# Gate and up of a hybrid decoder block: where the seven-product groups stand between the plain blocks

## The chip, the cores and the metric

The kernel runs on one core of one Trainium2 chip. The metric is the time on the device in microseconds (us), as the median of several executions. TensorE (PE) multiplies, VectorE (DVE) and ScalarE (ACT) prepare weights and take results out of PSUM, SyncE (SP) and GpSimd (POOL) issue transfers.

## The reference

One decoder layer on 256 tokens with 16 meta tokens in front, all in float32. The change lies in its last part, the gated feed-forward part:

```python
gate, up = jnp.split(_rms(h, n2) @ w_gu, 2, axis=-1)
return h + (jax.nn.silu(gate) * up) @ w_dn
```

`h` is 256 x 2048 here, `w_gu` is 2048 x 11264 (5632 columns of gate, 5632 of up) and `w_dn` is 5632 x 2048. All that comes before (RWKV-7 time mixing, forgetting attention, the gated merge and the output projection) stays as it is.

## The kernel before, in words

**Split weights.** Each float32 weight is turned into a high part `wh` (ACT copies and rounds it, line 343 or 518) and a low part `wl` (DVE subtracts the high part from the raw value, line 344 or 519). Activations are split the same way. A product is then three matmuls: high by high, high by low, low by high.

**Gate and up are cut into 11 strips of 512 columns.** Strips 0 to 7 (`PLAIN`) are done plainly. A strip has 8 gate blocks and then 8 up blocks (`plain_jobs`, `cm_jobs`). One plain block loads 256 rows of 512 weight columns and issues 16 matmuls on PE (lines 448, 449 and 451). So there are 128 plain blocks, numbered 0 to 127: gate of strip j is 16j to 16j+7 and up of strip j is 16j+8 to 16j+15. The 8 blocks of one gate or up add into four banks of PSUM, named `gt` or `up`, from the pool `main_ps`. After the last of the 8, `halves` (lines 455 and 456) takes the four banks out, and the next 8 blocks can open them again: this is what the title of the change calls a change of banks.

**Strips 8 to 10 (`BLOCK`) use a scheme with seven products** in place of eight on 2 x 2 sub-blocks (`block_jobs`). Gate of such a strip is one group (`bg8`, `bg9`, `bg10`), up another (`bh8`, `bh9`, `bh10`). A group goes through 8 channel pairs, and each pair is two pieces: a first piece with 9 matmuls (weights `fh`, `fl`) and a second one with 12 (weights `wh`, `wl` made from the raw tile `fr`), so 16 pieces in all. A group adds into four banks of the other pool, `aux_ps`; the first piece uses two of them, the second piece the other two. The second operands are sums of activations kept in eight tiles, `home0` to `home3` and four that lie in the rooms of the results of strips 6 and 7 (`homeh6`, `homel6`, `homeh7`, `homel7`, for channel pairs 4 to 7).

**After an up group** the function `turn` multiplies by the gate on DVE, then on PE transposes the result into two banks `bt` of the same pool `aux_ps` (line 403), and ACT and DVE split these into `ach` and `acl` (lines 518 and 519). Only then are the two banks free again. A pool gives a bank to a tile when its first instruction comes in the order of the program. The steps of `turn` are put off by a nominal clock (`LATER`, `FOLD`) which the matmuls move on, so they land some blocks later in the order.

**The table `SPANS` sets the order.** It has a row for each of the six groups: the plain block in front of which the first piece stands, the one in front of which the last piece stands, and the blocks that get no piece. Between these, one piece stands in front of each plain block. All five engines run in the order in which the program is written there (`manual_schedule`), and weights are made three jobs ahead of their matmuls (`AHEAD`), out of four buffers each for `wh` and `wl`.

**The down projection** comes after block 127. It adds the plain part into four banks `dn` (from `main_ps`) and the products of its own seven-product scheme into four banks `dnp` (from `aux_ps`), which are opened some 96 matmuls later. Up of strip 7 (`up7`, blocks 120 to 127) takes its banks from `aux_ps`, unlike the other strips.

Of the kernel before, what the change touches and what calls it, by code (L numbers as in the profile page):

```python
# [20 lines left out]
NMETA = 16  # L21

T = 256
# [4 lines left out]
DFF = 5632  # L28
# [13 lines left out]
for _n, _k in (("n1", 16), ("mu", 24), ("mu_w", 1), ("mu_a", 1), ("mu_g", 2), ("w0", 8), ("a0", 8), ("k_k", 8),  # L42
# [30 lines left out]
QUICK = [FAST[:-1], FAST]  # L73
PLAIN = list(range(8))
BLOCK = list(range(8, 11))
SPANS = ((8, 26, (11, 17, 21)), (28, 43, ()), (45, 62, (51, 59)), (64, 80, (75,)), (82, 99, (85, 93)),
         (101, 116, ()))
FOLD = 6000
AHEAD = 3
LATER = 2500  # L80
# [43 lines left out]
def hybrid_block(ctx, tc, A, out, dbg=None):  # L124
# [1329 lines left out]
    def plain_jobs(j):  # L1454
        gs = []
        rb = bcast(rsb2, 4)

        def post_gate(pss):
            g = gates_of(j)
            gs.append(g)  # L1460
            for m in range(4):
                halves(g[:, m], pss[m])

            def rest():
                nc.vector.tensor_tensor(g, g, rb, op=ALU.mult)
                yield LATER
                nc.scalar.activation(g, g, AF.Silu)
            spawn(rest(), LATER)

        def post_up(pss):  # L1470
            ub = gu.tile([P, 4, T], F32, tag="ub", name=f"ub{j}")
            for m in range(4):
                halves(ub[:, m], pss[m])

            def rest():
                nc.vector.tensor_tensor(ub, ub, gs[0], op=ALU.mult)
                yield LATER
                split(*act_of(j), ub)
                for i in range(2):
                    if 2 * j + i in FAST:  # L1480
                        yield (i + 1) * LATER
                        shape = "p (a n c) -> p a n c"
                        sr = room("l", BLOCK[-1], f"ss{2 * j + i}r", F32R).rearrange("p m c -> p (m c)")
                        ssd[2 * j + i] = yield from sums_of_tokens(sr.rearrange(shape, a=2, n=4), f"ss{2 * j + i}",
                                                                   ub[:, 2 * i], ub[:, 2 * i + 1], False)
            spawn(rest(), LATER)
        return (cm_jobs(wgu[:, j * 512:(j + 1) * 512], KT, hts, NMETA, T, post_gate, name=f"gt{j}")
                + cm_jobs(wgu[:, DFF + j * 512:DFF + (j + 1) * 512], KT, hts, NMETA, T, post_up, alloc=aux_ps if j == PLAIN[-1] else main_ps, name=f"up{j}"))

    def token(i, k, t):  # L1490
        at = NMETA + t * P
# [2 lines left out]
    def block_jobs(j):  # L1494
        gbs = []

        def group(col, post, name):
            box = []

            def mk(i):  # L1500
                src = wgu[i * 256:(i + 1) * 256, col + j * 512:col + (j + 1) * 512]
                first, end = i == 0, i == KT // 2 - 1
                raws = []

                def load0():
                    raw = gu.tile([P, 1024], F32, tag="fr", name="fr", bufs=2)
                    raws.append(raw)
                    rn = raw.rearrange("p (n c) -> p n c", c=256)
                    for k, to in enumerate((rn[:, 0::3], rn[:, 1:3])):
                        nc.sync.dma_start(to, src[k * P:(k + 1) * P, :].rearrange("p (x c) -> p x c", x=2))  # L1510
                    w = [gu.tile([P, 784], F32R, tag=t, name=t)[:, c:c + 768] for t, c in zip(("fh", "fl"), PLACE_T)]
                    split(*w, raw[:, :768])
                    b11, b21, b22, b12 = (raw[:, n * 256:(n + 1) * 256] for n in range(4))
                    nc.vector.tensor_tensor(rn[:, 0::3], rn[:, 0::2], bcast(b12, 2), op=ALU.subtract)
                    for o, x_, y_, op in ((b22, b22, b11, ALU.add), (b21, b21, b22, ALU.subtract)):
                        nc.vector.tensor_tensor(o, x_, y_, op=op)  # L1516
                    return w

                def load1():
                    w = [wp.tile([P, WCOLS], F32R, tag=t, name=t, bufs=WB)[:, c:c + 1024]  # L1520
                         for t, c in zip(("wh", "wl"), PLACE_T)]
                    split(*w, raws[0])
                    return w

                def product(at, a, w, n, opens=False, closes=False):
                    o = box[0][at]
                    hi, lo_ = (x_[:, n * 256:(n + 1) * 256] for x_ in w)
                    nc.tensor.matmul(o, a[0], hi, start=first and opens, stop=False, skip_group_check=True)
                    nc.tensor.matmul(o, a[1], hi, start=False, stop=False, skip_group_check=True)
                    nc.tensor.matmul(o, a[0], lo_, start=False, stop=end and closes, skip_group_check=True)  # L1530
                    slot(3 * 256 / 2.4)

                def s_of(n):
                    return tuple(homes[i][:, a, n, :] for a in range(2))

                def mul0(w):
                    if first:
                        b = [aux_ps(f"{name}{n}") for n in range(4)]
                        box.append({n: b[c // 2][:, (c % 2) * 256:(c % 2 + 1) * 256]
                                    for c, n in enumerate(("p1", "c12", "c11", None, "p7", "p5", "p6", "c21"))})  # L1540
                    product("p1", token(i, 0, 0), w, 0, True)
                    product("c12", s_of(3), w, 2, False, True)
                    product("c11", token(i, 1, 0), w, 1, True, True)

                def mul1(w):
                    product("p7", s_of(2), w, 3, True)
                    product("p5", s_of(0), w, 0, False, True)
                    product("p6", s_of(1), w, 2, True)
                    product("c21", token(i, 1, 1), w, 1, False, True)
                    if end:  # L1550
                        post(box[0])
                return [(load0, mul0), (load1, mul1)]
            return [mk(i) for i in range(KT // 2)]

        def sums(dst, ps, name):
            u, v = (gu.tile([P, 256], F32, tag=n, name=f"{name}{n}") for n in ("bu", "bv"))
# [20 lines left out]
        def post_up(ps):  # L1577
# [13 lines left out]
                for b, pt in enumerate(pts):  # L1591
                    split(*(t[:, 2 * b:2 * b + 2] for t in act_of(j)), pt.rearrange("p (m t) -> p m t", m=2))
            spawn(turn(), LATER)
        return [group(0, post_gate, f"bg{j}"), group(DFF, post_up, f"bh{j}")]

    def nudge(w):
        lo_ = w[0][1]
# [74 lines left out]
    def slow_jobs(i, cg, cs, end):  # L1672
        def mk(x_):
# [4 lines left out]

            def mul(w):
                if not cs:  # L1680
                    cs.extend(main_ps(f"dn{cg}{n}") for n in range(4))
                first = i == ORDER[cg][0]
                for t in range(2):
                    for k in range(2):
                        product(cs[2 * t + x_], a_of(i, k, t), w[0], k, first and k == 0, end and k == 1)
                    if end:
                        post(cg, t, x_, cs[2 * t + x_])
# [9 lines left out]
    def fast_jobs(i, cg, q, cs, ps, end):  # L1697
# [31 lines left out]

        def mul0(w):  # L1730
            if not ps:
                ps.extend(aux_ps(f"dnp{cg}{n}") for n in range(4))
            product(ps[0], a_of(i, 0, 0), w, 0, first, end)

        def mul1(w):
# [139 lines left out]
```

## Time and profile before

| | |
|---|---|
| median of 3 executions | 1523.97 us |
| the profiled execution, its own time | 1523.83 us |
| its span, first to last instruction | 1521.8 us |
| PE busy | 1500.7 us, 99% of the span |
| DVE busy | 1238.4 us, 81% |
| ACT busy | 842.3 us, 55% |
| first plain matmul of gate, first of down | 788.3 us, 1286.1 us |

Times in the rows are counted from the start of the span. Gate and up are the stretch from 788.3 to 1286.1 us. A row of the timeline gives the start, the duration, the engine and line, what is written and read, and, in square brackets, how long the engine stood idle in front of it and what ended that. A row of the waits gives who waited for whom, the sum, the number and the longest one.

### The profile page before, as it was taken

What the parts mean: (1) busy time and instruction counts of PE and PEld (TensorE: products, weight loads), DVE (VectorE), ACT (ScalarE), POOL (GpSimd) and SP (SyncE); (2) the same over time, 40 slices, a digit from 0 to 9 for tenths busy, and PEclk for the clock granted to TensorE, in tenths of its full rate; (3) what the DMA queues carried; (4) which work ended last, traced back from release to release, by engine and by line L of the source; (5) the groups of instructions that cost most, each with busy time, mean ns of one, the idle gap of its engine ahead of it and who ended that gap; (6) DMA issues with size and microseconds to landing.
All of it is one profiled execution on the core that took longest, in us unless ns stands there. A gap on an engine that the chain in (4) does not pass through costs nothing. (4 is left out here: it accounts for less than half of the span.)

```text
span 1521.8 us, 27095 instructions
## 1 busy us (share of the span) xinstructions
PE 1500.7 (99%) x10320; PEld 1344.1 (88%) x10320; DVE 1238.4 (81%) x2121; ACT 842.3 (55%) x1212; POOL 148.5 (10%) x263
## 2 busy tenths in 40 slices
PE   9999999999999999999999999999979999999998
PEld 9999999999989888998889999899969898887887
DVE  7888699689689757876777888889878986789987
ACT  7664565475465545544555555455545555555553
POOL 2112202302202100000002000000000001310000
PEclk9999999999999999999999999999989999999999
DMA  8567456646645757767879656476556656986662
GB/s 272 165 171 207 118 157 187 173 121 174 187 130 154 218 149 220 234 223 242 263 251 328 194 180 222 153 243 205 189 166 198 224 187 208 367 254 201 225 211 84
DMA packets 225123, 306.45 MB, mean 201 GB/s; under 512 B 26017, under 2 KB 148401, under 8 KB 224993
## 3 DMA queue, kind: packets, MB, share of 16 engines
q1 hardware_dynamic: 208960, 277.25, 59.1%
q0 software_dynamic: 9984, 20.98, 4.2%
q10 hardware_dynamic: 6048, 6.49, 1.2%
q8 instruction: 81, 1.33, 0.3%
q14 instruction: 50, 0.40, 0.1%
HBM read 285.90 MB, written 18.78 MB: 200 GB/s over the span
## 5 line engine op out<-in xcount | busy, mean ns | idle before, releaser
L344 DVE TENSOR_TENSOR wl<-raw,wh 128x1024 fp32r<-128x1024 f32 x402 | 490.4, 1227 | 123.7 <-ACT wh L343 116.9
L343 ACT ACTIVATE wh<-raw 128x1024 fp32r<-128x1024 f32 x402 | 423.9, 1057 | 281.9 <-PE br L374 38.0
L449 PE MATMUL up<-hts,wh 128*128 128x512 f32 x512 | 180.1, 395 | 2.4 <-DVE acl L519 2.0
L449 PE MATMUL zg<-xhl,wh 128*128 128x512 f32 x512 | 181.1, 399 | 0.0
L449 PE MATMUL gt<-hts,wh 128*128 128x512 f32 x512 | 179.6, 394 | 0.0
L451 PE MATMUL gt<-hts,wl 128*128 128x256 f32 x480 | 134.7, 281 | 0.0
L451 PE MATMUL up<-hts,wl 128*128 128x256 f32 x480 | 134.7, 281 | 0.0
L451 PE MATMUL zg<-xhl,wl 128*128 128x256 f32 x480 | 134.3, 280 | 0.0
L449 PEld LDWEIGHTS up<-hts,wh 128*128 128x128 f32 x512 | 95.0, 189 | 20.0 <-issue 2.3
L449 PEld LDWEIGHTS zg<-xhl,wh 128*128 128x128 f32 x512 | 94.3, 188 | 18.7 <-issue 0.7
L449 PEld LDWEIGHTS gt<-hts,wh 128*128 128x128 f32 x512 | 94.8, 188 | 17.1
L1663 PE MATMUL dn<-wh,ach 128*128 128x512 f32 x257 | 101.2, 394 | 0.0
L1664 PE MATMUL dn<-wh,acl 128*128 128x512 f32 x257 | 100.8, 392 | 0.0
L1665 PE MATMUL dn<-wl,ach 128*128 128x512 f32 x257 | 100.2, 392 | 0.4 <-DVE wl L344 0.4
L451 PEld LDWEIGHTS up<-hts,wl 128*128 128x128 f32 x480 | 91.4, 190 | 1.0
L451 PEld LDWEIGHTS gt<-hts,wl 128*128 128x128 f32 x480 | 91.1, 190 | 1.3 <-DVE wl L344 0.2
L451 PEld LDWEIGHTS zg<-xhl,wl 128*128 128x128 f32 x480 | 90.9, 189 | 1.2
L518 ACT ACTIVATE wh<-fr 128x1024 fp32r<-128x1024 f32 x48 | 50.9, 1061 | 63.4 <-DVE fr L1516 34.3
L518 ACT ACTIVATE wh<-tt 128x1024 fp32r<-128x1024 f32 x38 | 40.4, 1063 | 68.2 <-PE dn L1664 62.2
L373 PE MATMUL f<-xhl,wh 128*128 128x272 f32 x256 | 75.9, 296 | 0.0
L375 PE MATMUL f<-xhl,wl 128*128 128x272 f32 x256 | 73.6, 288 | 0.0
L374 PE MATMUL f<-xhl,wh 128*128 128x272 f32 x256 | 73.6, 288 | 0.0
(758 smaller groups left out, 3924.3 us busy)
## 6 DMA issues: line engine op xcount, KB each, us to landing
raw<-in_w_in_dram SPq DMA_DIRECT2D x160, 512.0 KB, 3.8
raw<-in_w_gate_up_dram SPq DMA_DIRECT2D x128, 512.0 KB, 4.9
raw<-in_w_down_dram SPq DMA_DIRECT2D x50, 512.0 KB, 4.8
fr<-in_w_gate_up_dram SPq DMA_DIRECT2D x96, 256.0 KB, 4.0
q<-in_w_down_dram SPq DMA_DIRECT2D x38, 512.0 KB, 6.7
raw<-in_w_o_dram SPq DMA_DIRECT2D x32, 512.0 KB, 5.5
raw<-in_w_branch_a_dram SPq DMA_DIRECT2D x16, 512.0 KB, 4.5
raw<-in_w_branch_b_dram SPq DMA_DIRECT2D x16, 512.0 KB, 3.9
```

The costliest lines, as they stand in the source:

```text
L343: nc.scalar.activation(th, rr, AF.Copy)
L344: nc.vector.tensor_tensor(tl, rr, th.bitcast(F32), op=ALU.subtract)
L373: nc.tensor.matmul(ps, wh, ah, start=first, stop=False)
L374: nc.tensor.matmul(ps, wh, al, start=False, stop=False)
L375: nc.tensor.matmul(ps, wl, ah, start=False, stop=last)
L449: nc.tensor.matmul(ps.rearrange("p (a t) -> p a t", a=2), wh, act, start=first, stop=last)
L451: nc.tensor.matmul(ps[:, :T], wl, act[:, 0, :], start=False, stop=False)
L518: nc.scalar.activation(hi, src, AF.Copy)
L1663: nc.tensor.matmul(o, a[0], hi, start=first, stop=False)
L1664: nc.tensor.matmul(o, a[1], hi, start=False, stop=False)
L1665: nc.tensor.matmul(o, a[0], lo_, start=False, stop=last)
```

## The change

Four rows of `SPANS` move. Between an up group and the next group there are now more plain blocks: `bh8` still ends in front of block 43, and `bg9` starts in front of block 48 and no longer 45; `bh9` ends in front of block 82 and not 80, and `bg10` starts in front of 87 and not 82. The last group, `bh10`, stands at blocks 106 to 121 and not 101 to 116, so that it crosses the change of banks from `gt7` to `up7`. It takes its channel pairs in the order 4, 5, 6, 7, 0, 1, 2, 3 (`turn=4`). `up7` takes its banks from `main_ps` like the others, and in down the two pools swap: `dn` from `aux_ps`, `dnp` from `main_ps`. No operation is added or dropped in gate, up and down.

```diff
-SPANS = ((8, 26, (11, 17, 21)), (28, 43, ()), (45, 62, (51, 59)), (64, 80, (75,)), (82, 99, (85, 93)),
-         (101, 116, ()))
+SPANS = ((8, 26, (11, 17, 21)), (28, 43, ()), (48, 64, (60,)), (66, 82, (75,)), (87, 104, (93, 99)),
+         (106, 121, ()))
...
-                + cm_jobs(wgu[:, DFF + j * 512:DFF + (j + 1) * 512], KT, hts, NMETA, T, post_up, alloc=aux_ps if j == PLAIN[-1] else main_ps, name=f"up{j}"))
+                + cm_jobs(wgu[:, DFF + j * 512:DFF + (j + 1) * 512], KT, hts, NMETA, T, post_up, name=f"up{j}"))
...
-        def group(col, post, name):
+        def group(col, post, name, turn=0):
             box = []
+            pairs = [(i + turn) % (KT // 2) for i in range(KT // 2)]
...
-                first, end = i == 0, i == KT // 2 - 1
+                first, end = i == pairs[0], i == pairs[-1]
...
-            return [mk(i) for i in range(KT // 2)]
+            return [mk(i) for i in pairs]
...
-        return [group(0, post_gate, f"bg{j}"), group(DFF, post_up, f"bh{j}")]
+        return [group(0, post_gate, f"bg{j}"), group(DFF, post_up, f"bh{j}", 4 if j == BLOCK[-1] else 0)]
...
-                    cs.extend(main_ps(f"dn{cg}{n}") for n in range(4))
+                    cs.extend(aux_ps(f"dn{cg}{n}") for n in range(4))
...
-                ps.extend(aux_ps(f"dnp{cg}{n}") for n in range(4))
+                ps.extend(main_ps(f"dnp{cg}{n}") for n in range(4))
```

**PE after the second up group.** `bt90` and `bt91` are the two banks of the transposed result of `bh9`; `bg100` to `bg103` are the four banks of `bg10`, the first two for its first pieces and the last two for its second pieces; `gt5_0` to `gt5_3` are the banks of the plain blocks beside them. Square brackets name the engines on which a row waits. Before, from the last matmul of the first piece to the second piece:

```order
L1530 MATMUL bg101_13250<-fl_13162,hts_9129 128x256
L449 MATMUL gt5_0_13197<-hts_9129,wh_13192 128x512 [waits Activation_49]
...
L451 MATMUL gt5_3_13200<-hts_9129,wl_13193 128x256
L403 MATMUL bt90_13293<-ident_69,hb9_13180 128x128 [waits DVE_49]
L403 MATMUL bt90_13293<-ident_69,hb9_13180 128x128 x3
L403 MATMUL bt91_13294<-ident_69,hb9_13180 128x128 x4
L1528 MATMUL bg102_13251<-wh_13219,home0_9974 128x256 [waits DVE_49]
```

After, from the transposes to the second piece:

```order
L403 MATMUL bt90_13337<-ident_69,hb9_13234 128x128 [waits DVE_49]
L403 MATMUL bt90_13337<-ident_69,hb9_13234 128x128 x3
L403 MATMUL bt91_13338<-ident_69,hb9_13234 128x128 x4
...
L449 MATMUL gt5_3_13152<-hts_9129,wh_13273 128x512
...
L1529 MATMUL bg100_13393<-fh_13297,hts_9129 128x256 [waits Activation_49]
...
L449 MATMUL gt5_3_13152<-hts_9129,wh_13326 128x512
L1529 MATMUL bg102_13395<-wh_13361,home0_9974 128x256 [waits DVE_49]
```

Before, the transposes stand right in front of the second piece of the next group. After, they stand 26 plain matmuls ahead of its first piece, and a further 9 and 16 ahead of its second piece; from the end of `bh9` to the transposes there are 54 plain matmuls. At the first up group it is the same count (54 and 26), and there neither piece of `bg9` waits on the transposed banks.

**DVE between the same two places.** `hb9` is the result of `bh9`, `ss8r` and `ss9r` are sums of activations for down, `ub4` is up of strip 4, `wl` and `fl` are low parts of weights, `acl9` is the split that frees the banks. Before:

```order
L1563 TENSOR_TENSOR hb9_13180<-bh92_12499,bh9bu_13181 128x256
L344 TENSOR_TENSOR wl_13193<-raw_13191,wh_13192 128x1024 [waits DMAHW1_49,Activation_49]
L1476 TENSOR_TENSOR ub4_13149<-ub4_13149,gates4_12838 128x1024
L1582 TENSOR_TENSOR hb9_13180<-hb9_13180,gates9_12427 128x1024 [waits DVE_49]
L519 TENSOR_TENSOR wl_13220<-fr_13158,wh_13219 128x1024 [waits Activation_49]
L519 TENSOR_TENSOR acl4_13232<-ub4_13149,ach4_13231 128x1024 [waits Activation_49]
L344 TENSOR_TENSOR wl_13245<-raw_13243,wh_13244 128x1024 [waits DMAHW2_49,PE_49,Activation_49]
...
L344 TENSOR_TENSOR wl_13327<-raw_13325,wh_13326 128x1024 [waits DMAHW6_49,PE_49,Activation_49]
L519 TENSOR_TENSOR acl9_13340<-bt90_13293,ach9_13339 128x512 [waits Activation_49]
```

After:

```order
L1564 TENSOR_TENSOR hb9_13234<-bh92_12552,bh9bu_13235 128x256
L344 TENSOR_TENSOR wl_13247<-raw_13245,wh_13246 128x1024 [waits DMAHW2_49,Activation_49]
L519 TENSOR_TENSOR ss8r_13220<-ss8r_13220 128x512 [waits Activation_49]
L1583 TENSOR_TENSOR hb9_13234<-hb9_13234,gates9_12480 128x1024 [waits DVE_49]
L344 TENSOR_TENSOR wl_13274<-raw_13272,wh_13273 128x1024 [waits DMAHW3_49,PE_49,Activation_49]
L519 TENSOR_TENSOR fl_13298<-fr_13294,fh_13297 128x768 [waits DMAHW5_49,DMAHW4_49,Activation_49]
...
L344 TENSOR_TENSOR wl_13327<-raw_13325,wh_13326 128x1024 [waits DMAHW6_49,PE_49,Activation_49]
L519 TENSOR_TENSOR ss9r_13314<-ss9r_13314 128x512 [waits Activation_49]
L519 TENSOR_TENSOR wl_13362<-fr_13294,wh_13361 128x1024 [waits PE_49,Activation_49]
L519 TENSOR_TENSOR acl9_13372<-bt90_13337,ach9_13371 128x512 [waits Activation_49]
```

In the rows left out of the second piece stand the two steps on `fr` (lines 1515 and 1517, three instructions) and four short sums into `ss9r`. The product and the split of `ub4` have moved ahead of the end of `bh9`, and so has most of `ss8r`.

**PE at the end of gate and up.** `up7_0` is the first bank of up of strip 7, `gt7_3` the last of the gate before it, `bh100` and `bh101` banks of the last group, `bt100` and `bt101` its transposed result. Before:

```order
L403 MATMUL bt100_14796<-ident_69,hb10_14702 128x128 [waits DVE_49]
L403 MATMUL bt100_14796<-ident_69,hb10_14702 128x128 x3
L403 MATMUL bt101_14797<-ident_69,hb10_14702 128x128 x4
...
L449 MATMUL gt7_3_14532<-hts_9129,wh_14714 128x512
L449 MATMUL up7_0_14831<-hts_9129,wh_14741 128x512 [waits Activation_49]
...
L449 MATMUL up7_2_14833<-hts_9129,wh_14741 128x512 [waits DVE_49,PE_49]
```

After:

```order
L449 MATMUL gt7_3_14446<-hts_9129,wh_14683 128x512
L1529 MATMUL bh100_14174<-fh_14700,hts_9129 128x256 [waits Activation_49]
...
L1531 MATMUL bh101_14175<-fl_14701,hts_9129 128x256
L449 MATMUL up7_0_14791<-hts_9129,wh_14724 128x512 [waits DVE_49]
...
L403 MATMUL bt101_14922<-ident_69,hb10_14830 128x128 x4
...
L1664 MATMUL dn00_15043<-wh_15026,ach0_10597 128x512 [waits Activation_49]
```

Before, the third bank of `up7` waits for the split of `bt10`. After, each bank of `up7` waits for the banks of `gt7`, behind one piece of the last group, and 58 plain matmuls of `up7` stand between `bt10` and the first matmul of down, which waits only for its own weights.

## The prediction, made blind

> **What bounds the kernel now.** The first view is the page: which engine is full, and where it is not.
>
> ```profile
> PE 1500.7 (99%) x10320; PEld 1344.1 (88%) x10320; DVE 1238.4 (81%) x2121; ACT 842.3 (55%) x1212; POOL 148.5 (10%) x263
> PE   9999999999999999999999999999979999999998
> PEclk9999999999999999999999999999989999999999
> ```
>
> PE is the bound nearly everywhere. One slice falls to 7 tenths, and the granted clock dips in the same slice. As the change adds and drops no operation, it can only move what PE waits for. The second view is therefore the list of PE's waits; each row has the sum in us, the number and the longest.
>
> ```profile
> PE bg L1528 <- DVE acl L519: 11.7, 2, 8.8
> PE up L449 <- DVE acl L519: 2.0, 1, 2.0
> PE up L449 <- DVE gates L456: 0.4, 1, 0.4
> PE dn L1665 <- DVE wl L344: 0.4, 1, 0.4
> ```
>
> The first two rows are one and the same thing: a matmul needs a bank that the transposed result of an up group still holds, and the bank comes free when DVE has made `acl`. The third row is an ordinary change of banks of the plain blocks. What the waits cost in all is read from PE's timeline, where a wait stands in brackets. The rows below are the starts of pieces and blocks; the ones between them are left out.
>
> ```profile
> 947.48 0.28 PE L1528 MATMUL bh<-wh,homel 128*128 128x256 f32 x1
> 948.89 0.40 PE L449 MATMUL up<-hts,wh 128*128 128x512 f32 x1
> ...
> 954.45 0.28 PE L1528 MATMUL bg<-fh,hts 128*128 128x256 f32 x1
> 955.51 0.39 PE L449 MATMUL up<-hts,wh 128*128 128x512 f32 x1
> ...
> 958.30 1.03 PE L403 MATMUL bt<-ident,hb 128*128 128x128 f32 x8
> ...
> 962.21 0.38 PE L1528 MATMUL bg<-wh,home 128*128 128x256 f32 x1 [2.88 <-DVE acl L519]
> 964.35 0.63 PE L449 MATMUL up<-hts,wh 128*128 128x512 f32 x1
> ...
> 968.06 0.28 PE L1528 MATMUL bg<-fh,hts 128*128 128x256 f32 x1
> ```
>
> The first four rows give the normal prices. A second piece takes 948.89 - 947.48 = 1.41 us, two plain blocks take 954.45 - 948.89 = 5.56, so 2.78 each, and a first piece takes 955.51 - 954.45 = 1.06. Around the wait it is otherwise: the second piece takes 964.35 - 962.21 = 2.14 and the plain block after it 968.06 - 964.35 = 3.71. So a wait costs more than its own length. The windows show why; their columns are length, busy time with instructions of PE, its weight loads, DVE, ACT and POOL, then the granted clock, the share of DMA and GB/s.
>
> ```profile
> 963.10:966.30 3.20, 3.20 (x14) 2.91 (x14) 0.78 (x1) 1.06 (x1) 0.00 (x0) 0.50 0.69 234
> 1116.40:1119.90 3.50, 3.43 (x15) 3.33 (x16) 0.61 (x2) 0.61 (x1) 0.00 (x0) 0.50 0.59 234
> ```
>
> After each of the two waits of `bg` PE runs at a granted clock of 0.50 for 3.2 to 3.5 us. The other two places where PE waited:
>
> ```profile
> 1116.47 0.58 PE L1528 MATMUL bg<-wh,home 128*128 128x256 f32 x1 [8.78 <-DVE acl L519]
> 1119.20 0.63 PE L449 MATMUL gt<-hts,wh 128*128 128x512 f32 x1
> ...
> 1122.36 0.28 PE L1528 MATMUL bg<-fh,hts 128*128 128x256 f32 x1
> ...
> 1261.62 0.39 PE L449 MATMUL up<-hts,wh 128*128 128x512 f32 x1
> ...
> 1286.06 0.40 PE L1663 MATMUL dn<-wh,ach 128*128 128x512 f32 x1
> ```
>
> **What the waits cost.** First group: 2.88 idle, + (2.14 - 1.41) + (3.71 - 2.78) = 4.5 us. Second: 8.78 idle, + (1119.20 - 1116.47 - 1.41) + (1122.36 - 1119.20 - 2.78) = 8.78 + 1.32 + 0.38 = 10.5 us. Third: `up7` has eight plain blocks and nothing else, 8 x 2.78 = 22.24, and takes 1286.06 - 1261.62 = 24.44, so 2.2 us, of which 2.0 is the wait. In all 17.2 us, or 17.6 with the 0.4 of the third row of the waits.
>
> Here a rule of the Trainium skill can be weighed (TensorE: Matmul & The Clock Gate, Part 1: The HAM clock gate): the clock halves after an idle window of about 3.4 us and comes back after about as long a busy one. By that rule the wait of 2.88 us would carry no slow stretch, the sum would be 1.7 us less, and the time 1508.3. The trace disagrees: the clock was 0.50 behind this wait, so the 4.5 stands.
>
> **First and second up group: will the banks be free in time?** What matters is the way on PE from the end of the up group to the first matmul that needs a transposed bank, against the work that DVE must do until `acl`. By the order of the changed kernel, PE does 54 plain matmuls (3.375 blocks, 9.4 us), the transposes (1.0), 26 plain matmuls (4.5), the first piece (1.1) and one block (2.8): 18.8 us from the end of `bh9` to the second piece of `bg10`, the first that waits. For DVE the timeline of before, around the worst wait, has every kind of step with its price from start to start; its first row is PE's, where `bh9` has just ended.
>
> ```profile
> 1097.25 0.40 PE L449 MATMUL gt<-hts,wh 128*128 128x512 f32 x1
> ...
> 1097.18 0.96 DVE L519 TENSOR_TENSOR fl<-fr,fh 128x768 fp32r<-128x768 f32 x1 [0.31 <-ACT fh L518]
> 1098.17 0.69 DVE L1514 TENSOR_TENSOR fr<-fr 128x512 f32<-128x512 f32 x1
> 1098.90 0.89 DVE L1516 TENSOR_TENSOR fr<-fr 128x256 f32<-128x256 f32 x2
> 1099.70 0.42 DVE L1563 TENSOR_TENSOR hb<-bh,bh9bu 128x256 f32<-128x256 f32 x1
> ...
> 1102.61 1.22 DVE L344 TENSOR_TENSOR wl<-raw,wh 128x1024 fp32r<-128x1024 f32 x1
> 1103.74 1.22 DVE L1476 TENSOR_TENSOR ub<-ub,gates 128x1024 f32<-128x1024 f32 x1
> 1104.87 1.22 DVE L1582 TENSOR_TENSOR hb<-hb,gates 128x1024 f32<-128x1024 f32 x1
> 1106.01 1.22 DVE L519 TENSOR_TENSOR wl<-fr,wh 128x1024 fp32r<-128x1024 f32 x1
> ...
> 1111.93 0.28 DVE L1332 TENSOR_TENSOR ss8r<-ub 128x128 f32<-128x128 f32 x1
> ...
> 1112.86 1.22 DVE L344 TENSOR_TENSOR wl<-raw,wh 128x1024 fp32r<-128x1024 f32 x1
> 1113.99 0.68 DVE L519 TENSOR_TENSOR ss8r<-ss8r 128x512 fp32r<-128x512 f32 x1
> 1114.60 1.22 DVE L344 TENSOR_TENSOR wl<-raw,wh 128x1024 fp32r<-128x1024 f32 x1
> 1115.73 1.28 DVE L519 TENSOR_TENSOR acl<-bt,ach 128x512 fp32r<-128x512 f32 x2
> ```
>
> In the changed order DVE has, from the sums of `bh9` to `acl9`: the sums (1102.61 - 1099.70 = 2.91), a `wl` (1.13), the split of `ss8r` (0.61), the product (1.14), a `wl` (1.13), one `fl` with its steps on `fr` (0.99 + 0.73 + 0.80), the sums of `ss9r` (1112.86 - 1111.93 = 0.93), a `wl` (1.13), the split of `ss9r` (0.61), the `wl` of the first second piece (1.13) and `acl9` (1.28). That is 14.5 us. Before, `bh9` ended at 1097.25 and its sums started 2.45 us later; with as much delay it is 17.0. Against 18.8 the margin is 1.8 to 4.3 us, so I take the wait as gone.
>
> At the first group the list is shorter, without `ss8r` and `ss9r`: 2.91 + 1.13 + 1.14 + 1.13 + 2.52 + 1.13 + 1.13 + 1.28 = 12.4, or 14.8 with the delay, and no piece of `bg9` waits for `acl8` at all. What can be late there is the change from `up2` to `gt3`, whose first bank is taken out by DVE right behind `acl8`: needed at 9.4 + 1.0 + 4.5 + 1.1 = 16.0, ready at 12.8 to 15.2. So 4.5 us are gone too, with a margin of at least 0.8.
>
> ACT is the other queue that is passed. It runs in order and stood still before the worst wait:
>
> ```profile
> 1112.97 0.63 ACT L518 ACTIVATE ss8r<-ss8r 128x512 fp32r<-128x512 f32 x1 [4.29 <-DVE ss8r L1334]
> ...
> 1114.46 1.06 ACT L518 ACTIVATE ach<-bt 128x512 fp32r<-128x512 f32 x2
> ```
>
> The copy of `bt` stood behind the split of `ss8r`, and that behind DVE. In the changed order the split of `ss9r` is in that place, and DVE gets to it 10.4 to 12.8 us after the end of `bh9`; that split (0.63), a copy of 1024 columns (as long as the two `ach` of 512, 1.06) and the first `ach` (0.5) follow, 12.6 to 15.0. DVE reaches `acl9` at 13.3 to 15.7, so ACT adds nothing to the 17.0.
>
> **The end.** `up7` no longer asks for a bank of `bt10`: its 2.2 us go. Instead it asks for the banks of `gt7`, behind one piece (1.06 us). That is the wait of the third row, bounds 0 and 0.4; since every change of banks but one went without a wait, I take 0 for the new one and let the old 0.4 stand, which covers both. `dn` now takes the banks that `bt10` used, but 58 matmuls of `up7` (3.6 blocks, 10.1 us) lie between, and in the first group the piece that `acl` released started 2.9 us behind the end of the transposes (962.21 - 958.30 - 1.03); `dnp` opens `up7`'s banks 96 matmuls into down. Both are covered by PE's own work. The turned order makes the last group read the rooms of strips 6 and 7 at blocks 106 to 113, ahead of what is written into them: `ach6` behind block 111, `gates7` behind 119. So ACT does not stand there; if it did, three jobs made ahead (2 x 2.78 + 1.4 = 7 us) would cover PE. The loads follow their blocks in SP's queue, in the same number, and POOL's transfers of sums move with their steps; no wait of PE's list ends with either.
>
> **Sum.** 1523.83 of the profiled execution - 4.5 - 10.5 - 2.2 = 1506.6; the median stood 0.1 above it: 1506.7 us.
>
> **The rivals.** What DVE carries and how PE runs without waits is in three windows of before:
>
> ```profile
> 780.00:957.00 177.00, 177.00 (x1121) 159.97 (x1120) 148.35 (x209) 99.66 (x123) 10.01 (x19) 1.00 0.70 226
> 970.00:1105.00 135.00, 135.00 (x878) 123.15 (x878) 119.13 (x170) 76.65 (x97) 2.14 (x4) 1.00 0.62 199
> ```
>
> (1) *A rest of the wait stays at the second group.* If `acl9` takes as long as before, 1117.0 - 1097.25 = 19.8 us, PE waits 1.0 and the time is 1507.7. If ACT's 4.29 comes on top of the 17.0, it is 21.3, a wait of 2.5, and with the slow stretch of the first group (1.7) 4.2: 1510.9. For it: none of the quoted rows of DVE behind the first, to 1117, has a bracket, so it never stood idle. Against: the product on `ub4` (1.13) and its split have left this stretch.
>
> (2) *Bank changes turn into waits.* `up7` and `dn` now both follow a change of banks on a pool just used. Two waits as at the first group cost 2 x 4.5 = 9.0: 1515.7. Against it: from 970 to 1105 lie five changes of banks, and PE was busy for 135.00 of 135.00 us. The Trainium skill (TensorE: Matmul & The Clock Gate, A second HAM failure mode: psum-queue depth-cycling) speaks for this rival: cycling through banks makes short idles that swing the clock. The clock of 1.00 in that window disagrees.
>
> (3) *The waits only move, since DVE is the bound.* DVE was busy 119.13 of 135 us, 88%, where PE never waited; the third group has one block without a piece less than before, which takes 2.78 - 1.13 = 1.65 us of room. If DVE were the limit, PE would gain only the 2.2 of `up7` and the two slow stretches (1.7 each): 1518.2 to 1521.6. Against: 12% of room.
>
> (4) *Slower: the clock.* Without waits PE runs at full load from 788 to the end, some 715 us. If such a load lowers the granted clock, a clock of 0.97 over it adds 21 us to 1506.7: 1528. It decides against the change from a mean clock of 0.976 on (17.2 of 715). Against: 177 us on end without a gap at 1.00, and down after that at 9 tenths or more in the page.
>
> **How the numbers follow.** Forecast 0.80, (1) 0.09, (2) 0.05, (3) 0.04, (4) 0.02. The forecast's own bounds are 1506.3 (the 0.4 goes as well) and 1507.5 (two small waits of 0.4). The range takes in rival (1) above, and 1.3 us below for what one profiled execution doesn't show: 1505.0 to 1511.5. A difference of 2%, some 30 us, is about what a measurement of this kernel tells from no change; all idle and slow time of PE in gate and up is under 18 us, so none of the cases gets there but for something unseen: faster by over 2% 0.01, slower 0.01, within it 0.98.
>
> **What would show it.** Right: in the list of PE's waits both rows that end with `acl` are gone, the granted clock is 1.00 in every window of gate and up, `up7` takes 22.2 to 22.7 us from its first matmul to the first of down, and down starts near 1269. Step by step: the transposes of `bh8` and `bh9` stand amid plain matmuls and `acl` ends before the next group's second piece; no row has `dn` or `dnp` waiting for `acl` or `ub`. Wrong: a row `bg` on `acl` of over 1 us (1), rows of `up` on `gates` or `gt` on `ub` of over 2 us (2), many rows of PE on `wl` or `fl` (3), or a window of full PE with a clock under 0.98 (4).

## The result, and the profile after

The changed kernel takes 1510.27 us (median of 4 executions, 1510.01 to 1510.8), the kernel before beside it 1523.97 us. The ratio is 0.9909, with a 95% interval of 0.989 to 0.9928: a gain of 0.9%. The forecast was 1506.7 us, with a range of 1505.0 to 1511.5. The gain is 13.7 us by the medians and 13.1 us by the spans (1521.8 and 1508.7), where 17.2 us were expected. One of the four executions of the kernel before took 2449.2 us and is left out of its median (with it, the median is 1524.39), and its single runs beside the experiments went up to 1526.45 us. So the experiments below are compared by one stretch of their traces: from the first plain matmul of gate to the first matmul of down, called the stage. What lies outside it takes 1023.6 to 1024.2 us in every kept trace but one (1025.3, the experiment with only the third group moved).

The page of the changed kernel, and from the list of PE's waits the rows from gate to down (sum in us, number, longest):

```profile
PE 1497.8 (99%) x10320; PEld 1340.9 (89%) x10320; DVE 1238.9 (82%) x2121; ACT 840.6 (56%) x1212; POOL 150.5 (10%) x263
PE   9999999999999999999999999999999999999998
PEclk9999999999999999999999999999999999999999
```

```profile
PE up L449 <- DVE gates L456: 1.4, 1, 1.4
PE gt L451 <- DVE wl L344: 1.2, 2, 0.8
PE up L451 <- DVE wl L344: 0.8, 1, 0.8
PE dn L1666 <- DVE wl L344: 0.4, 1, 0.4
```

The slice at 7 tenths and the dip of the clock are gone, and so are all rows in which PE waits for `acl` (11.7 and 2.0 us before). The last row stood there before too. The other three are new: a change of banks that waits for the sums of `gates`, and three plain blocks whose `wl` is late.

The windows give the balance of the stage. The first row is the kernel before, the second the changed one, the third the best variant of the experiments (length, then busy time of PE, its weight loads, DVE, ACT and POOL, clock, DMA share, GB/s):

```profile
788.30:1286.06 497.76, 483.71 (x3092) 439.09 (x3090) 417.05 (x587) 274.41 (x341) 15.35 (x29) 0.99 0.65 209
```

```profile
788.55:1273.05 484.50, 481.02 (x3092) 436.30 (x3091) 416.89 (x587) 273.17 (x341) 15.67 (x29) 1.00 0.66 214
```

```profile
788.19:1268.28 480.09, 479.82 (x3092) 436.25 (x3090) 416.54 (x587) 273.17 (x341) 15.23 (x29) 1.00 0.67 216
```

The third row shows what PE needs nearly without waits and without slow clock: 479.8 us for the same 3092 matmuls. Against that, the kernel before lost 497.76 - 479.82 = 17.9 us. Of these, 497.76 - 483.71 = 14.05 are idle, and in 3.9 PE counts as busy, mostly at the slow clock. The changed kernel still loses 484.50 - 479.82 = 4.7 us, of which 3.5 idle. In the other 1.2 PE counts as busy at a clock of 1.00: the matmuls beside a wait have longer rows, so that PE is 1.3 us late behind the wait of 0.77 at 1040. So the old losses are gone whole, and new ones of 4.7 us have come: 17.9 - 4.7 = 13.2.

The new waits, in the timeline of PE after the change:

```profile
1040.65 0.39 PE L451 MATMUL gt<-hts,wl 128*128 128x256 f32 x1 [0.77 <-DVE wl L344]
...
1045.23 0.39 PE L451 MATMUL gt<-hts,wl 128*128 128x256 f32 x1 [0.45 <-DVE wl L344]
...
1122.08 0.50 PE L449 MATMUL up<-hts,wh 128*128 128x512 f32 x1 [1.44 <-DVE gates L456]
...
1196.42 0.39 PE L451 MATMUL up<-hts,wl 128*128 128x256 f32 x1 [0.76 <-DVE wl L344]
```

Two of them, at 1040 and 1196, lie some 12 us behind the end of `bg9` (group 3) and of `bg10` (group 5). The wait at 1122 is the change of banks at block 88. What leads to the first is seen on DVE, and then on ACT:

```profile
1025.47 0.42 DVE L456 TENSOR_TENSOR ub<-ub,up 128x256 f32<-128x256 f32 x1
...
1030.81 0.42 DVE L1564 TENSOR_TENSOR gates<-bg,bg9bu 128x256 f32<-128x256 f32 x1
...
1034.85 1.22 DVE L1476 TENSOR_TENSOR ub<-ub,gates 128x1024 f32<-128x1024 f32 x1
...
1039.36 1.23 DVE L344 TENSOR_TENSOR wl<-raw,wh 128x1024 fp32r<-128x1024 f32 x1 [0.94 <-PE bh L1531]
```

```profile
1036.10 1.06 ACT L518 ACTIVATE ach<-ub 128x1024 fp32r<-128x1024 f32 x1 [4.03 <-DVE ub L1476]
1037.06 1.32 ACT L1573 ACTIVATE gates<-gates,rs 128x512 f32<-128x512 f32 x2
1038.29 1.04 ACT L343 ACTIVATE wh<-raw 128x1024 fp32r<-128x1024 f32 x1
```

`bg9` now ends in front of block 64, and block 64 is itself a change of banks. So on DVE the taking out of `up3` (from 1025.47), the sums of `bg9` (from 1030.81) and the product for strip 3 (1034.85) follow on one another, where before `bg9` ended two blocks earlier. ACT runs in order: it stands 4.03 us for that product, then makes `ach`, then the two silu activations of `bg9` (1.32 us), and only then the next `wh`. That `wh` ends at 1038.29 + 1.04 = 1039.33, and the `wl` of the block starts at 1039.36; PE gets to it first. The bracket of that `wl` names a matmul of `bh`, which ends at about the same time (1039.36), so this trace alone doesn't tell which of the two held it. That it is the order of ACT's steps was tried by experiment (below).

The second group, where the forecast had its narrowest margin, in rows of PE and of DVE after the change:

```profile
1100.44 0.40 PE L449 MATMUL gt<-hts,wh 128*128 128x512 f32 x1
...
1109.81 1.03 PE L403 MATMUL bt<-ident,hb 128*128 128x128 f32 x8
...
1119.05 0.28 PE L1529 MATMUL bg<-wh,home 128*128 128x256 f32 x1
```

```profile
1102.33 0.42 DVE L1564 TENSOR_TENSOR hb<-bh,bh9bu 128x256 f32<-128x256 f32 x1
...
1112.90 0.29 DVE L1332 TENSOR_TENSOR ss9r<-ub 128x128 f32<-128x128 f32 x1 [1.07 <-DMA ss<-ss8r]
...
1116.76 1.28 DVE L519 TENSOR_TENSOR acl<-bt,ach 128x512 fp32r<-128x512 f32 x2
```

`bh9` ends at 1100.44. `acl9` is ready at 1116.76 + 1.28 = 1118.04, and the second piece starts at 1119.05 with no wait: 1.0 us to spare. In the third row of PE the piece starts 18.6 us behind the end of `bh9`.

The end of gate and up, from the first matmul of `up7` to the first of down:

```profile
1248.50 0.39 PE L449 MATMUL up<-hts,wh 128*128 128x512 f32 x1
...
1251.29 0.28 PE L1529 MATMUL bh<-wh,home 128*128 128x256 f32 x1
...
1252.72 0.39 PE L449 MATMUL up<-hts,wh 128*128 128x512 f32 x1
...
1262.09 1.03 PE L403 MATMUL bt<-ident,hb 128*128 128x128 f32 x8
...
1262.88 0.48 PE L449 MATMUL up<-hts,wh 128*128 128x512 f32 x1
...
1273.05 0.40 PE L1664 MATMUL dn<-wh,ach 128*128 128x512 f32 x1
```

No bracket stands at the change of banks to `up7` nor at the one to `dn`. The stretch takes 24.55 us: a last second piece (1252.72 - 1251.29 = 1.43), the transposes (0.79) and 22.33 for the eight blocks.

### The profile page after: what moved, and what is told of

It reads as the page before. It is cut to its first block, busy times and chain, and to the rows that moved or that the text cites. A ratio compares the mean times of both kernels' runs of the same rounds, so it can differ in the third digit from the quotient of the medians.

```text
span 1508.7 us, 27083 instructions
## 1 busy us (share of the span) xinstructions
PE 1497.8 (99%) x10320; PEld 1340.9 (89%) x10320; DVE 1238.9 (82%) x2121; ACT 840.6 (56%) x1212; POOL 150.5 (10%) x263
## 4 chain that ended last, share of the span: by engine, by line
PE 74%; issue 19%; DVE 3%; DMA 2%; ACT 1%; POOL 0%; SPq 0%; DVEq 0%; POOLq 0%; ACTq 0%
PE zg L449 8%; PE dn L1666 4%; PE dn L1664 4%; PE dn L1665 4%; PE zg L451 4%; PE up L449 3%; PE f L449 2%; PE br L373 2%; PE br L374 2%; PE br L375 2%; PE f L373 2%; PE wo L1362 2%; PE gt L449 2%; PE wo L1363 2%; PE wo L1364 2%
```

## The experiments

**The theory** after the result: the new waits come because the ends of two gate groups (`bg9`, `bg10`) fell on a change of banks (blocks 64 and 104), where the sums of the group, the taking out of a plain strip and its product meet on DVE, and ACT stands behind them. **The rivals:** DVE is the bound and any gain at one place is paid at another (rival 3 of the forecast); or the new waits belong to the moved last group and the swapped pools.

**The end alone.** The rows of `SPANS` for the first groups go back, the last group stays at the new place.

```diff
-... (48, 64, (60,)), (66, 82, (75,)), (87, 104, (93, 99)), (106, 121, ()))
+... (45, 62, (51, 59)), (64, 80, (75,)), (82, 99, (85, 93)), (106, 121, ()))
```

> The first five groups stand as in the kernel before; only the last group (blocks 106 to 121, turned pairs), the banks of up7 and the swap in down are the new ones. Theory (each wait has its own cause, and each part of the change removes its own): only the 2.2 us of up7 go, so about 13.76 - 11.6 = 2 us under the kernel before; both waits of bg on acl stay with 2.9 and 8.8 us, with a slow clock behind each, and no wait of up on gates at block 120. Rival (VectorE sets the pace and waits only move): the time stays within 1 us of the kernel before, with new small waits of PE near the end.

It took 1526.07 us, the kernel before beside it 1526.22, where a gain of 2 was expected. The stage is 500.5 us, 2.7 more than in the trace of the kernel before (an execution of 1523.83 us; of the one of 1526.22 no trace was kept). The list of PE's waits in gate and up:

```profile
PE bg L1529 <- DVE acl L519: 11.7, 2, 8.8
PE up L449 <- DVE gates L456: 3.8, 1, 3.8
```

The waits of `bg` are those of before, and the wait at the end (2.0) is gone. The 3.8 us are new. With `bg10` ending in front of block 99 and `bh10` starting in front of 106, no piece stands in front of block 104, which is a change of banks: PE goes from the last plain block of `gt6` straight to `up6`, and that needs the banks that DVE is still emptying. A slow clock behind the wait, for 3.0 us at 0.50, cost about 1.5 us on top. This was a flaw of the experiment, and it shows what a change of banks costs without a piece in front of it.

**The end alone, with a piece in front of every change of banks.** As above, with the last group from 104 on:

```diff
-         (106, 121, ()))
+         (104, 121, (109, 117)))
```

> The first five groups as in the kernel before, and the new end again, but the last group now at blocks 104 to 121 (no piece at 109 and 117), so that the change of banks at block 104 has a piece in front of it; in the run with 106 to 121 it had none, and up waited 3.8 us for gates there. Theory: that wait belongs to the missing piece; it falls to 0.4 or less, the two waits of bg on acl stay (2.9 and 8.8), up7 to down takes 22.3: 2.2 to 2.9 us under the kernel before. Rival (the new end itself brings the wait): a wait of over 2 us of up on gates stays at block 104 or comes at 120.

1520.53 us, beside 1524.11 for the kernel before; the stage 494.6 us, 3.2 less than before. The only wait left in gate and up is that of `bg` on `acl` (11.6 in two, the longest 8.7). So the missing piece was the cause of the 3.8, and the change of the end by itself is worth about 3 us: the 2.2 of `up7` and the old wait on `gates` of 0.4 with what follows it. The moved last group and the swapped pools bring no wait of their own.

**The first group back, the second as changed.**

```diff
-... (48, 64, (60,)), (66, 82, (75,)), (87, 104, (93, 99)), ...
+... (45, 62, (51, 59)), (64, 80, (75,)), (87, 104, (93, 99)), ...
```

> The changed kernel with its third and fourth group back at 45 to 62 and 64 to 80; the second gap and the end stay new. Theory: the first wait of bg on acl is back, 2.9 us idle and 4.5 us with the slow stretch; the end of the third group is two blocks ahead of a change of banks again, so the two waits of gt on wl behind block 66 (0.8 and 0.4, 2.1 us with the slow matmuls around them) go: 1510.3 + 4.5 - 2.1 = 1512.7. The second wait of bg stays away. Rival (VectorE sets the pace): the time stays within 1 us of 1510.3, since the waits only change places.

1512.77 us, the stage 487.1 us, 2.6 more than the changed kernel.

```profile
PE bg L1529 <- DVE acl L519: 2.9, 1, 2.9
PE up L449 <- DVE gates L456: 1.5, 1, 1.5
PE up L451 <- DVE wl L344: 0.8, 1, 0.8
```

The first old wait is back, with its slow clock: 4.5 us. Yet the time rises by 2.6 only, since the two waits of `gt` on `wl` (1.2) are gone with what surrounds them: `bg9` ends in front of block 62 here, two blocks ahead of the change of banks. The wait of `up` on `wl`, behind the end of `bg10` at 104, stays. That is the theory's reading, and the time is the one that was expected, 1512.7.

**The second group near again, the rest as changed.**

```diff
-... (66, 82, (75,)), (87, 104, (93, 99)), (106, 121, ()))
+... (66, 82, (75,)), (84, 101, (90, 96)), (106, 121, ()))
```

> The changed kernel with its fifth group at 84 to 101, two blocks behind the fourth group as before. Theory: bg10's second piece needs the banks about 10.4 us behind the end of bh9, and acl9 came 17.6 us behind it in the changed kernel: a wait of 7.2 us, about 1.7 more for the slow clock; the waits of up on gates at block 88 (1.4, 1.7 with the rest) and of up on wl near block 106 (0.8, 1.3 with the rest) go, since the group no longer begins or ends at a change of banks: 1510.3 + 8.9 - 3.0 = 1516.2. Rival (VectorE sets the pace): within 1 us of 1510.3.

1521.88 us, the stage 496.1 us, 11.6 more than the changed kernel; about 6 was expected.

```profile
PE bg L1529 <- DVE acl L519: 7.4, 1, 7.4
PE up L449 <- DVE gates L456: 2.2, 1, 2.2
...
PE gt L451 <- DVE wl L344: 1.2, 2, 0.8
```

The wait for `acl` is as long as forecast, 7.4 against 7.2. What was missed is that block 104 is again without a piece, as in the first experiment: 2.2 us of wait. Slow clock follows on both waits and costs more than the 1.7 us that were put for it: PE runs at 0.50 for 5.9 us behind the first and for 3.4 us behind the second, which costs about 2.8 and 1.7 us. The waits of `gt` on `wl` are there again, as `bg9` ends at 64. The wait of `up` on `wl` is gone, as `bg10` ends at 101, and so is the one at block 88.

**Ends of gate groups away from the changes of banks.** All four groups are placed so that no gate group ends on a change of banks and the changes of banks at 64 and 104 still have a piece in front. `acl` has nearly as much time as in the changed kernel.

```diff
-SPANS = ((8, 26, (11, 17, 21)), (28, 43, ()), (48, 64, (60,)), (66, 82, (75,)), (87, 104, (93, 99)),
-         (106, 121, ()))
+SPANS = ((8, 26, (11, 17, 21)), (28, 43, ()), (47, 62, ()), (64, 81, (68, 75)), (86, 102, (94,)),
+         (104, 121, (109, 117)))
```

> Groups three to six at 47 to 62, 64 to 81, 86 to 102 and 104 to 121: gaps of four and five blocks behind the up groups, but no group ends in front of a block that follows a change of banks, so that the sums of a gate group and the halves and products of a plain group no longer meet on VectorE and in ScalarE's queue. Theory (the new waits come from that meeting): the waits of gt and up on wl and of up on gates go, at most 1 us of new ones: 1510.3 - 4 to 5 = 1505.5 to 1507. Rival (VectorE has too little room wherever the groups stand): as much waiting elsewhere, 1509 to 1511; or bg10 waits for acl9 by 1 to 2 us, which shows as bg on acl.

1507.41 us, the stage 481.5 us, 3.0 less than the changed kernel. One row is left in gate and up:

```profile
PE up L449 <- DVE gates L456: 1.4, 2, 1.0
```

All waits on `wl` have gone, as expected, and none on `acl` has come. The change of banks at block 88 still waits, 1.0 us.

**Only the third group away from the change of banks.**

```diff
-... (48, 64, (60,)), (66, 82, (75,)), ...
+... (47, 62, ()), (64, 82, (68, 75, 79)), ...
```

> The changed kernel with only the third and fourth group moved: 47 to 62 and 64 to 82 (no piece at 68, 75, 79), so that the third group ends two blocks ahead of the change of banks at 64. Theory (the end of a gate group and a change of banks meet): the two waits of gt on wl behind block 66 go (2.1 us with what is around them), the waits of up at 88 (1.4) and near 106 (0.8) stay: 1510.3 - 2.1 = 1508.2. The gap of four blocks, 43 to 47, brings no wait of bg on acl. Rival (VectorE has too little room): the 1.2 us of waiting come back elsewhere, 1510.

1508.8 us, the stage 481.7 us. The two waits of `gt` on `wl` are gone, and the wait of `up` on `wl` at the end of `bg10` stays with 0.8: the waits at the two ends are independent. The wait of `up` on `gates` at block 88 was expected to stay at 1.4, but it fell to 0.7; the experiment with a room of its own, below, shows what that wait hangs on.

**Only the silu steps of the gate groups later.** The places of the groups stay as in the changed kernel. The two activations of `gates` (line 1573) get a later due time, so that ACT makes the `wh` in front of them.

```diff
-            spawn(rest(), 2 * LATER)
+            spawn(rest(), 6 * LATER)
```

> The changed kernel with one number changed: the two activations on the gate of a seven-product strip (1.3 us on ScalarE) are put off by six steps of the nominal clock and not two, so that they no longer stand in ScalarE's queue in front of the weights that are late. Theory (ScalarE's queue, held up for 4.0 us by a step that waits for VectorE and then by these activations, makes wh late): the waits of gt and up on wl of 0.8 us at 1039 and 1195 go, with 2 x 1.3 us in all; the one of 0.5 at 1044 and the 1.4 at block 88 may stay: 1507.5 to 1508. Rival (VectorE's own work makes wl late): both waits stay, 1510.3.

1507.04 us, the stage 481.1 us, 3.4 less than the changed kernel. PE's waits in gate and up, and ACT at the end of `bg9`:

```profile
PE gt L451 <- DVE wl L344: 0.5, 1, 0.5
PE up L449 <- DVE gates L456: 0.3, 1, 0.3
```

```profile
1035.71 1.06 ACT L518 ACTIVATE ach<-ub 128x1024 fp32r<-128x1024 f32 x1 [4.03 <-DVE ub L1476]
1036.68 1.04 ACT L343 ACTIVATE wh<-raw 128x1024 fp32r<-128x1024 f32 x1
```

ACT stands as long as in the changed kernel (4.03), but the `wh` comes right behind `ach`: 0.97 us after its start (1036.68 - 1035.71), and not 2.19 (1038.29 - 1036.10). The `wl` behind it starts at 1037.95, while PE is still in the piece of `bh` that the bracket named (1037.39 to 1038.98), so that piece was not what held it. Both waits of nearly 0.8 are gone from the list, the one at 1040 and the one at 1196. DVE does the same work in a shorter stage, so its amount of work was not what held PE there. The wait at block 88 fell as well, from 1.4 to 0.3. So not all of the 3.4 us belongs to the two activations: 1.2 of it is the shorter wait at block 88, some 2.2 the waits on `wl` with what surrounds them. Timed in five rounds beside the kernel before, the same kernel takes 1507.9 us (1506.79 to 1508.21), a ratio of 0.9889 (0.9874 to 0.9904). That is 2.4 us under the changed kernel, where 3.2 were expected, and not within 1 us of it, as the rival had it:

> The same kernel as the one with only the activations put off, timed. Theory: 1507.0, 0.9885 of the kernel before and 3.2 us under the changed kernel. Rival: the one look was a lucky one, and it lies within 1 us of 1510.3.

**The wait at block 88: is it a copy on ACT?** In this theory `bg10`'s first pieces stand too close to block 88. A block without a piece is put in front of it, into the variant with the ends apart.

```diff
-... (86, 102, (94,)), ...
+... (86, 102, (89,)), ...
```

> The kernel with the ends of groups apart (1507.4), with the fifth group's block without a piece at 89 and not at 94. Theory: at block 88 ScalarE's copies of gates stood behind a copy of fr weights that waits for VectorE's steps on fr; without a piece at 89 they stand behind a plain copy, so the wait of up on gates there (1.0 us) falls to 0.3 or less: 1506.5. Rival (VectorE is too far behind at that place whatever ScalarE does): the wait stays at 1 us or over.

1507.2 us, the stage 481.4 us; `up` still waits for `gates`, 1.5 us in two, the longest 1.2. The theory falls. In the trace of this kernel DVE stood 1.4 us for the outgoing transfer of `ss8r`, as it did for 1.07 us in the changed kernel (1112.90, quoted above): `ss9r`, the sums for the next strip, uses the same room, and can't be written before the transfer has read it.

**A room of its own for `ss9r`.** The changed kernel, with one allocation changed, so that `ss8r` and `ss9r` don't share a room:

```diff
-sr = room("l", BLOCK[-1], f"ss{2 * j + i}r", F32R).rearrange("p m c -> p (m c)")
+sr = room("h" if 2 * j + i in (5, 7, 9) else "l", BLOCK[-1], f"ss{2 * j + i}r", F32R).rearrange("p m c -> p (m c)")
```

> The changed kernel with the sums ss5r, ss7r and ss9r in a room of their own, so that ss9r no longer waits until the transfer has read ss8r out of the shared one. Theory: VectorE stood 1.07 us for that transfer in front of block 88, and the 1.4 us that PE waits for gates there come mostly from it: VectorE's wait goes and PE's falls to 0.3 to 0.4; 1510.3 - 1.1 = 1509.2; the waits on wl at 1039, 1044 and 1195 stay. Rival (VectorE is too far behind at that place anyway): PE's wait there stays at 1 us or over, 1510.3.

1509.43 us; the stage 483.3 us, 1.2 less than the changed kernel. PE's waits in gate and up, and the first sum of `ss9r` on DVE:

```profile
PE gt L451 <- DVE wl L344: 1.2, 2, 0.8
PE up L451 <- DVE wl L344: 0.8, 1, 0.8
PE up L449 <- DVE gates L456: 0.2, 1, 0.2
```

```profile
1111.56 0.28 DVE L1332 TENSOR_TENSOR ss9r<-ub 128x128 f32<-128x128 f32 x1
```

The second fence is the step of DVE that stood 1.07 us before: it has no bracket now. The wait of 1.4 at block 88 falls to 0.2, and the other waits are as they were. So the transfer was the cause of that wait. The other traces in which `bg10` starts just ahead of block 88 agree: DVE stands for the transfer 1.83, 1.35, 1.07, 1.01, 0.28, 0 and 0 us (first group back, spare block, changed, ends apart, third group apart, silu later, the best variant below), and PE waits at block 88 for 1.53, 1.17, 1.44, 1.02, 0.65, 0.27 and 0.27 us.

**The best of them.** The third group apart, and the silu steps later:

```diff
-... (48, 64, (60,)), (66, 82, (75,)), ...
+... (47, 62, ()), (64, 82, (68, 75, 79)), ...
...
-            spawn(rest(), 2 * LATER)
+            spawn(rest(), 6 * LATER)
```

> The third and fourth group apart from the change of banks (47 to 62 and 64 to 82) and the two activations on the gate put off by six steps. Theory: the causes add; of the waits in gate and up that were left when the activations alone were put off (0.5 at 1043 with 0.7 in all, 0.3 at block 88 with 0.5 in all) the first goes, the second stays or goes: 1507.0 - 0.7 to 1.3 = 1505.7 to 1506.3, with PE waiting less than 0.5 us in gate and up. Rival (waits only move once VectorE has so little room): 1507 or more.

1506.07 us in five rounds (1505.76 to 1506.84), the kernel before 1524.25: a ratio of 0.988, with an interval of 0.9863 to 0.9896. The stage is 480.1 us; the one wait left in gate and up:

```profile
PE up L449 <- DVE gates L456: 0.3, 1, 0.3
```

This is 1.2% under the kernel before, and 4.2 us below the changed kernel's median; the two were timed in different sessions, beside a kernel before of 1524.25 and of 1523.97 us, and their stages differ by 4.4 us.

| kernel | time, us | stage, us | waits in gate and up, us |
|---|---|---|---|
| before | 1523.97 | 497.8 | 11.7 and 2.0 `acl`, 0.4 `gates` |
| changed | 1510.27 | 484.5 | 1.4 `gates`, 2.0 `wl` |
| end alone | 1526.07 | 500.5 | 11.7 `acl`, 3.8 `gates` |
| end alone, covered | 1520.53 | 494.6 | 11.6 `acl` |
| first group back | 1512.77 | 487.1 | 2.9 `acl`, 1.5 `gates`, 0.8 `wl` |
| second group near | 1521.88 | 496.1 | 7.4 `acl`, 2.2 `gates`, 1.2 `wl` |
| ends apart | 1507.41 | 481.5 | 1.4 `gates` |
| ends apart, spare block | 1507.2 | 481.4 | 1.5 `gates` |
| third group apart | 1508.8 | 481.7 | 0.7 `gates`, 0.8 `wl` |
| silu later | 1507.9 | 481.1 | 0.3 `gates`, 0.5 `wl` |
| own room | 1509.43 | 483.3 | 0.2 `gates`, 2.0 `wl` |
| third apart, silu later | 1506.07 | 480.1 | 0.3 `gates` |

## Why the prediction was right, and where it was off

**The number: inside the range, outside the forecast's own bounds.** The time of 1510.27 us is 3.6 above the forecast and lies outside the bounds that the forecast gave itself (1506.3 to 1507.5). It lies in the range since the range was opened for rival (1), which did not come. That the range held is luck; that the old waits go is not. The change stays within 2%, as forecast.

**The old waits: right.** Gone as forecast are both waits of `bg` and the one of `up7`. The sum of 17.2 us, or 17.6 with the wait on `gates`, is 17.9 by the windows. The parts agree where they were tried alone: putting the second group near again costs 7.4 us of wait where 7.2 was expected, and the end by itself is worth 3.2 us, where 2.2 and 0.4 stood.

**The margin at the second group: right in sign, narrower than stated.** PE's way was put at 18.8 us and took 18.6. DVE's way to `acl9` was put at 14.5 to 17.0 and took 1118.04 - 1100.44 = 17.6. Its sums started 1.9 us behind `bh9` (1102.33), which gives 14.5 + 1.9 = 16.4, and 1.07 us is the wait for the transfer of `ss8r`. The forecast had said that POOL's transfers "move with their steps" and that none of PE's waits ends with them. It had missed that DVE itself waits for one.

**The end: right, with a slip in the figure for proof.** "22.2 to 22.7" for `up7` to down had left out that a piece (1.43) and the transposes (0.79) now stand in that stretch. Without them it is 22.33, so no wait. Down starts at 1273.05 and not near 1269: that is the 4 us of new waits ahead of it.

**The step that failed** is the term for new waits: "I take 0 for the new one and let the old 0.4 stand". What came is 4.7 us. It was mis-sized in the first place because only the banks at the moved gaps were followed. Where the moved groups end was not: at blocks 64 and 104, on a change of banks. There the steps that both parts put off (the functions `rest`) and the taking out of the banks (`halves`) meet on DVE and ACT, and the `wh` of the next blocks waits in ACT's queue. The rest of it is the room that `ss8r` and `ss9r` share. The runs set the price: with all ends away from the changes of banks the stage is 3.0 us shorter, with the silu steps later 3.4 (1.2 of it at block 88), and with a room of its own 1.2. These shares overlap and are not to be added; the best variant takes off 4.4 of the 4.7.

**Rival (1)**, a rest of the wait at the second group, did not come: its price of 1.0 to 4.2 us would have given a like time, yet the trace has no wait there. **Rival (2)**, changes of banks that wait, is right in kind but not at its places, `up7` and `dn`, which went without a wait. It came at block 88 with 1.4 us, most of it by way of the transfer, and in two experiments at block 104 with 3.8 and 2.2. No swing of the clock came with it in the changed kernel, 1.00 over the stage; the Trainium skill's rule on cycling through banks (TensorE: Matmul & The Clock Gate, A second HAM failure mode: psum-queue depth-cycling), which spoke for this rival, had no effect here. **Rival (3)**, DVE as the bound, is refuted, though its sign, rows of PE on `wl`, came with three waits of 0.8 us and less: DVE does the same 417 us of work in a stage of 480.1 us. **Rival (4)**, a lower clock at full load, did not come: 1.00 over 484.5 us, and over 480.1 us in the best variant.

## What to carry to other kernels

When a group of work is moved to widen a gap, look at both of its ends: what is issued at an end (sums, products, activations) moves with it, and may fall on steps that another part issues there. Of an engine that runs in order, ask what stands in its queue behind a long wait. Here two activations that nobody needed soon, made ahead of a weight copy that the bound engine needed, brought two waits of PE. And a buffer that two steps share through an outgoing transfer is a wait of its own, to be listed beside the banks.

## What was not expected of the hardware

**Short waits bring a slow clock, in pieces of 3.41 us.** In gate and up, each wait of PE of 2.16 us or more that these traces have brought a stretch at a granted clock of 0.50. By windows of 0.2 us these stretches last 3.4 us (waits of 2.16, 2.88 and 3.77 us), 6.8 us (a wait of 8.74) or 10.2 us (waits of 7.37 and 8.78): one, two or three times 3.41. Only what lies behind the wait costs time, 3.0 to 5.9 us at half the clock. The windows of the experiment with the second group near, from its wait of 2.2 us on:

```profile
1192.60:1195.10 2.50, 0.38 (x3) 0.06 (x1) 1.68 (x5) 0.85 (x4) 0.00 (x0) 1.00 1.02 379
1195.60:1196.20 0.60, 0.60 (x5) 0.55 (x4) 0.48 (x2) 0.60 (x1) 0.00 (x0) 0.78 0.29 109
1196.20:1198.00 1.80, 1.80 (x7) 1.51 (x7) 1.56 (x2) 1.15 (x2) 0.00 (x0) 0.50 0.00 0
```

The first window holds the wait (PE is busy for 0.38 of 2.50 us); the clock falls some 0.8 us after PE went on. In the kernel before, the wait of 1.98 us in front of `up7` has no such thing behind it:

```profile
1265.10:1266.00 0.90, 0.85 (x5) 0.79 (x6) 0.90 (x2) 0.00 (x0) 0.00 (x0) 1.00 0.79 155
1266.00:1268.00 2.00, 2.00 (x13) 1.74 (x12) 0.94 (x2) 1.29 (x2) 0.00 (x0) 1.00 0.67 232
```

The Trainium skill (TensorE: Matmul & The Clock Gate, Part 1: The HAM clock gate) has the clock halve after an idle window of about 3.4 us; here 2.16 and 2.88 us of wait were enough and 1.98 and 1.44 were not. The measurement decides; the length of the slow stretches agrees with that window. Where a stretch begins is not fixed by the wait: behind the same wait of 2.88 us it began 0.7, 1.6 and 0.4 us after PE went on (before, end alone, end alone covered), and 0.3 us ahead of that with the first group back. So a wait's place against such a window may count as well as its length; that was not tried and stays open.

**A transfer of the same size takes longer or shorter.** The outgoing transfer of `ss8r`, issued by POOL, landed after 5.5 us in the changed kernel and after 4.2 us with the silu steps later. In both, `ss9r` came up on DVE some 4.5 us after the issue, so the 1.2 us that the later silu steps took off the wait at block 88 hang on the landing. Why it landed sooner is open.
